# Order at stage edges in a two-layer decoder trunk: PSUM banks of the mLSTM dealt anew, first heads and sums of squares begun some steps later, the last norm's weights on ScalarE

## The chip, the cores and the metric

The kernel runs on one core of a Trainium2 chip. The metric is the device time of one execution in microseconds (us), for which the median of several runs is given. The engines are TensorE (PE in the profile, with its weight loads as PEld), VectorE (DVE), ScalarE (ACT), GpSimd (POOL) and SyncE (SP, which issues most of the weight transfers). Each runs its own instructions in a fixed order and waits for the others by semaphores. TensorE writes into eight PSUM banks of 128 x 512 fp32.

## The reference

512 tokens of width 1024 run through two layers, then a last RMSNorm. Everything is fp32.

```python
def rmsnorm(x, g):
    y = xf * lax.rsqrt(jnp.mean(xf * xf, axis=-1, keepdims=True) + EPS)
    return (y * g.astype(jnp.float32)).astype(x.dtype)

def sqrelu_mlp(h, w1, w2):
    return jnp.square(jax.nn.relu(h @ w1)) @ w2
...
    for layer in range(DEPTH):
        if layer % N_MIXERS == 0:
            mix = diff_attention(rmsnorm(h, attn_norm[j]), ...)
        else:
            mix = mlstm_mixer(rmsnorm(h, mlstm_norm[j]), ...)
        h = h + mix.astype(h.dtype)
        h = h + sqrelu_mlp(rmsnorm(h, mlp_norm[layer]), mlp_w1[layer], mlp_w2[layer]).astype(h.dtype)
    return rmsnorm(h, final_norm)
```

The differential attention has 8 heads of two score maps each (width 64), a softmax with a bias by relative position, the difference of the two maps times the values, and a norm per head. The mLSTM has 4 heads of width 128 for q and k (after a causal convolution of width 4 and SiLU) and 256 for the values, with input and forget gates, a norm per head and an output gate. The MLP's inner width is 4096.

## The kernel before

Activations lie with the features on the partitions: `h[k]`, k = 0 to 7, is 128 features x 512 tokens. An fp32 product is made of three matmuls on rounded halves: an operand is split into a high part `hi` (a ScalarE copy) and a rest `lo` (a VectorE subtraction), and hi x hi, lo x hi and hi x lo are added up in a bank. `mm3` (L400 to L402) does so for 512 tokens at a time, `vpair_mm` (L432 to L434) for products with the tokens on the partitions, `down` (L922 to L924) for the second product of the MLP, and `finish` (L1285 to L1287) for its last 256 features together with the last norm. The weights come as tiles `raw`, and are split into `whi` (ScalarE) and `wlo` (VectorE, L528) ahead of their use.

RMSNorm is not applied before a product but after it. `operand` (L508 on) multiplies `h[k]` with the norm's weights while it splits it into `x_xh` (ScalarE) and `x_xl` (VectorE, L513), and `square_in` (L518) squares `h[k]` on ScalarE and adds it to `acc` on POOL (L524). `token_scale` later splits `acc` into `sh` and `sl`, sums over the partitions with two matmuls with a constant (`sums`, L535 and L536), and makes `rs`, the factor of each token, from the sum: VectorE L559, three ScalarE steps, VectorE L552, L553 and L561. The products are multiplied with `rs` when they are read out of the banks. For products with tokens on the partitions `token_cols` transposes `rs` (L569).

The order of TensorE is the program's. Most products call `tick()` after each step (three matmuls), and `after(n, fn)` runs `fn` n ticks later, so that scores, sums and transposes are put between the steps of the big products. The constants T_... are such distances: T_RS for the sums of the attention's norm, T_RSC for its transposes, T_CONST for L636 to L682 (the bias table's rows and the heads' mixing factors, with a transfer `rows` between), T_ONE and T_TWO for the first two heads' scores (L730), T_M and T_H for the first mLSTM head and the distance between heads, T_MRS for the sums of the mLSTM's norm. The orders of VectorE, ScalarE, POOL and SyncE are set by a scheduler when the kernel is built, so a moved matmul can move their instructions too; at run time they are fixed.

`banks(mm=3, sc=2, ac=3)` deals the eight PSUM banks to three uses: `mm` for products, `sc` for scores and sums, `ac` for what is summed up longer. The list it deals from, `idle`, has the bank that was given out longest ago first. Within a use the banks go round. `four(True)`, with which the mLSTM's gate products begin (`vpair_mm(x, 264)`), takes one `mm` bank and the three `ac` banks.

In the mLSTM's `head`, L1106 spreads the gates into a bank, VectorE (L1109) and ScalarE read it into `e_e`, POOL masks it, L1117 to L1119 make the scores, and VectorE multiplies both (L1120). L1140 on are the products with the values.

In the last MLP `finish` takes the place of the last `down`. It makes the last 256 features of the sum `h` tile by tile (two tiles, j = 0 and 1, for two halves of the tokens, i = 0 and 1). `early_sums` puts the sums of squares of the other 768 features (L1249, L1250) into two banks; `tail` adds those of the last 256, and `scaled` (L1262 on) makes the factor and multiplies. The norm's weights, times -0.5, are multiplied into `h` in between: six whole tiles in L1253 and the last two in halves in L1258.

Of the kernel before, what the change touches and what calls it, by code (L numbers as in the profile page):

```python
# [14 lines left out]
AF = mybir.ActivationFunctionType  # L15
ALU = mybir.AluOpType
# [6 lines left out]
KT = D // P  # L23
# [15 lines left out]

T_RS, T_RSC, T_CONST, T_BIAS, T_ROWS = 24, 39, 31, 4, 14
T_ONE, T_TWO = 3, 12


D_ATT = [
# [8 lines left out]
]  # L55


T_M, T_H = 15, 22
D_MLS = [(5, 8, 6), (5, 7, 9), (5, 9, 10), (7, 8, 12)]

T_GATES, T_GROWS, T_GCOLS, T_MRS = 3, 22, 56, 9
# [124 lines left out]
def trunk(ctx: ExitStack, tc, xT, wgt, wgt2, cols, rows, rel, consts, outT):  # L186
# [18 lines left out]
    def banks(**tags):  # L205

        free = list(idle)
        for tag, n in tags.items():
            turn[tag], free = free[:n], free[n:]
# [15 lines left out]
    mm = nc.tensor.matmul  # L225
    vec = nc.vector
    pool = nc.gpsimd
# [22 lines left out]
    def act(out, x, func, **kw):  # L250
        name = {AF.Exp: LNSET, AF.Ln: LNSET, AF.Sigmoid: SGSET}.get(func)
        if name:
            tables(name)
        ins = nc.scalar.activation(out, x, func, **kw)  # L254
        if name:
            behind(ins, loaded["load"])
            loaded["uses"].append(ins)
# [238 lines left out]
    def col(c):  # L496
        return colt[:, c : c + 1]
# [17 lines left out]
            square_in(k, acc)  # L515
        return lambda: (hi, lo)

    def square_in(k, acc):  # L518
        if k == 0:
            act(acc, h[k], AF.Square)  # L520
        else:
            s = tmp()
            act(s, h[k], AF.Square)
            pool.tensor_tensor(acc, acc, s, op=ALU.add)  # L524

    def split(src, hi, lo, eng=None):
        act(hi, src, AF.Copy)
# [35 lines left out]
    def scale_tile(name):  # L563
        return cp.tile([P, T], F32, tag=name, name=nm(name))
# [276 lines left out]
    def mlp(x, acc, g0, finish=None):  # L841
        with ExitStack() as st:
# [49 lines left out]
            def down(q, i):  # L892
# [53 lines left out]
                for n in (2 * i, 2 * i + 1):  # L946
                    if g0 is not None:
                        nxt.append(operand(n, g0, nacc))
                    else:
                        if n == 0:  # L950
                            finish.acc = acc_tile()
                        square_in(n, finish.acc)

            after(T_MLP, lambda: token_scale(acc, rs))
            ps = group_mm(x)
# [24 lines left out]

    def mlstm(x, acc):
        with ExitStack() as st:
            banks(mm=3, sc=2, ac=3)
            gp = Buffers(tc, st, name="gp", bufs=1)
            qp = Buffers(tc, st, name="qp", bufs=16)
            sg = Buffers(tc, st, name="sg", bufs=8)
# [248 lines left out]
    def finish(operands):  # L1235
# [10 lines left out]
        def early_sums():  # L1246
            split(acc, sh, sl)
            for s, c in zip(stat, (slice(0, H), slice(H, T))):
                mm(s[:, :H], ones_d, sh[:, c], start=True, stop=False)  # L1249
                mm(s[:, :H], ones_d, sl[:, c], start=False, stop=False)  # L1250

        for k in range(KT - 2):
            vec.tensor_scalar(h[k], h[k], col(C_FN + k), -0.5, op0=ALU.mult, op1=ALU.mult)  # L1253

        def tail(n, c, s):
            vec.tensor_tensor(h[n][:, c], part[n - pair[0]][:, c], h[n][:, c], op=ALU.add)
            act(s, h[n][:, c], AF.Square)
            vec.tensor_scalar(h[n][:, c], h[n][:, c], col(C_FN + n), -0.5, op0=ALU.mult, op1=ALU.mult)  # L1258

        def scaled(c, stat, ss):  # L1260
            for s in ss:
# [16 lines left out]
        for i, c in enumerate((slice(0, H), slice(H, T))):  # L1278
            ss = [tmp()[:, :H] for _ in pair]
            for j, n in enumerate(pair):  # L1280
                hi, lo = units[j]
                for k in range(KT):
                    w = slice(k * P, (k + 1) * P)
                    a, b = operands(k, i)
                    mm(part[j][:, c], hi[:, w], a, start=k == 0, stop=False)  # L1285
                    mm(part[j][:, c], hi[:, w], b, start=False, stop=False)
                    mm(part[j][:, c], lo[:, w], a, start=False, stop=k == KT - 1)  # L1287
                    tick()
                tail(n, c, ss[j])
                if i == 0 and j == 0:  # L1290
                    early_sums()
            if i == 0:
                after(T_FIN, lambda c=c, ss=ss: scaled(c, stat[0], ss))
            else:
                scaled(c, stat[1], ss)
# [94 lines left out]
```

## Time and profile before

| | us |
|---|---|
| runs | 1194.72, 1195.81, 1197.52 |
| median | 1195.81 |
| the profiled execution's own time | 1194.34 |
| its span, with a mean TensorE clock of 0.983 | 1192.3 |
| VectorE busy, 77% of the span | 919.9 |
| ScalarE busy, 51% | 603.0 |
| POOL busy, 16% | 189.2 |

The page's other rows of use are those that cut the span into 40 slices; each digit is a busy share in tenths, and PEclk is the clock that TensorE was granted:

```profile
PE   7899999999999999999989899999999999999994
PEclk9899999999999999999989999999999999999997
```

A slice is some 30 us. TensorE is busy nearly everywhere; the slices below 9 are the first two, the last, and the 21st and 23rd, around 610 and 670 us. A busy share of 9 at a clock of half speed is also lost time, which is why both rows are read together. The four places that the change touches are the start of the attention (26 to 60 us), the step from the first MLP to the mLSTM (593 to 617), the mLSTM's heads (640 to 805) and the last norm (1157 to 1192).

### The profile page before, as it was taken

How to read it: one execution, taken by the hardware profiler on the slowest of the kernel's cores; microseconds unless marked ns; L12 is line 12 of the kernel's file. 1: busy time of each engine (PE TensorE's matmuls, PEld its weight loads, DVE VectorE, ACT ScalarE, POOL GpSimd, SP SyncE). 2: the span in 40 equal slices, each digit the busy share in tenths (PEclk: the TensorE clock that was granted, in tenths of full speed). 3: DMA queues.
4: the chain of work that ended last, by engine and by line, in shares of the span. 5: the costliest groups of instructions: out<-in, count | busy, mean ns of one | idle time of the engine just before them, and what ended most of it. 6: DMA issues, size and time to landing. Idle time of an engine off the chain costs nothing.

```text
span 1192.3 us, 17221 instructions
## 1 busy us (share of the span) xinstructions
PE 1147.5 (96%) x6730; PEld 1011.2 (85%) x6730; DVE 919.9 (77%) x1387; ACT 603.0 (51%) x909; POOL 189.2 (16%) x180
## 2 busy tenths in 40 slices
PE   7899999999999999999989899999999999999994
PEld 5778888888998998989877789888889889899894
DVE  7789888587967957867989857766697686786884
ACT  5577776564534534434544537654453353443441
POOL 4432332130000000000221312223000000000011
PEclk9899999999999999999989999999999999999997
DMA  6622222233263362461222221223325526426312
GB/s 202 198 71 71 75 85 71 71 124 111 66 190 112 89 176 89 111 191 53 83 71 70 76 83 54 57 85 107 110 84 136 171 67 162 139 67 185 89 32 71
DMA packets 36592, 123.91 MB, mean 104 GB/s; under 512 B 4351, under 2 KB 6418, under 8 KB 36512
## 3 DMA queue, kind: packets, MB, share of 16 engines
q1 hardware_dynamic: 30288, 103.38, 27.0%
q0 software_dynamic: 5104, 17.87, 7.7%
q10 hardware_dynamic: 1120, 1.57, 0.4%
q8 instruction: 53, 0.87, 0.3%
q14 instruction: 27, 0.22, 0.1%
HBM read 108.11 MB, written 4.74 MB: 95 GB/s over the span
## 4 chain that ended last, share of the span: by engine, by line
PE 78%; DVE 14%; ACT 3%; issue 3%; DMA 2%; POOL 1%; DVEq 0%; SPq 0%; POOLq 0%; ACTq 0%
PE bank L401 15%; PE bank L402 15%; PE bank L400 15%; PE bank L923 7%; PE bank L924 7%; PE bank L922 7%; DVE wlo L528 2%; PE bank L432 2%; PE bank L433 1%; PE bank L434 1%; DVE tmp_tmp L1030 1%; DMA raw<-wgt 1%; DVE x_xl L513 1%; PE bank L730 1%; ACT whi L254 1%
## 5 line engine op out<-in xcount | busy, mean ns | idle before, releaser
L402 PE MATMUL bank<-x_xh,wlo 128*128 128x512 f32 x640 | 255.4, 399 | 1.3 <-DVE wlo L528 1.3
L401 PE MATMUL bank<-x_xl,whi 128*128 128x512 f32 x640 | 254.8, 398 | 1.0 <-DVE x_xl L513 1.0
L400 PE MATMUL bank<-x_xh,whi 128*128 128x512 f32 x640 | 254.0, 397 | 1.4 <-ACT whi L254 1.4
L254 ACT ACTIVATE whi<-raw 128x1024 fp32r<-128x1024 f32 (+2 forms) x128 | 133.4, 1042 | 120.9 <-PE bank L923 48.1
L528 DVE TENSOR_TENSOR wlo<-raw,whi 128x1024 fp32r<-128x1024 f32 (+2 forms) x128 | 161.9, 1265 | 35.2 <-ACT whi L254 34.6
L922 PE MATMUL bank<-uh,whi 128*128 128x256 f32 x560 | 157.9, 282 | 0.0
L924 PE MATMUL bank<-uh,wlo 128*128 128x256 f32 x560 | 157.8, 282 | 0.0
L923 PE MATMUL bank<-ul,whi 128*128 128x256 f32 x560 | 157.8, 282 | 0.0
L400 PEld LDWEIGHTS bank<-x_xh,whi 128*128 128x128 f32 x640 | 122.8, 192 | 28.8 <-ACT whi L254 2.1
L402 PEld LDWEIGHTS bank<-x_xh,wlo 128*128 128x128 f32 x640 | 121.1, 189 | 29.3 <-DVE wlo L528 2.4
L401 PEld LDWEIGHTS bank<-x_xl,whi 128*128 128x128 f32 x640 | 121.5, 190 | 28.3 <-DVE x_xl L513 1.4
L922 PEld LDWEIGHTS bank<-uh,whi 128*128 128x128 f32 x560 | 106.0, 189 | 0.1
L923 PEld LDWEIGHTS bank<-ul,whi 128*128 128x128 f32 x560 | 105.7, 189 | 0.3
L924 PEld LDWEIGHTS bank<-uh,wlo 128*128 128x128 f32 x560 | 105.8, 189 | 0.0
L943 POOL DMA_DIRECT2D h<-work x24 | 20.8, 866 | 511.1 <-DVE work L940 391.5
L254 ACT ACTIVATE uh<-chains 128x1792 fp32r<-128x1792 f32 (+1 forms) x35 | 55.6, 1590 | 57.8 <-DVE chains L883 57.7
L528 DVE TENSOR_TENSOR ul<-chains,uh 128x1792 fp32r<-128x1792 f32 (+1 forms) x35 | 66.0, 1886 | 23.7 <-ACT uh L254 23.4
L524 POOL TENSOR_TENSOR acc_acc<-acc_acc,tmp_tmp 128x512 f32<-128x512 f32 x33 | 54.6, 1654 | 170.8 <-ACT tmp_tmp L254 169.7
L432 PE MATMUL bank<-whi,x_xh 128*128 128x256 f32 (+1 forms) x256 | 73.9, 289 | 7.1 <-DVE work L939 5.7
L876 DVE SCALAR_TENSOR_TENSOR tmp_tmp<-bank,rs_rs 128x512 f32<-128x512 f32 x64 | 44.1, 689 | 45.9 <-PE bank L402 45.5
L254 ACT ACTIVATE whi<-wsums 128x1024 fp32r<-128x1024 f32 x47 | 49.8, 1059 | 51.5 <-PE bank L923 30.3
L433 PE MATMUL bank<-wlo,x_xh 128*128 128x256 f32 (+1 forms) x256 | 73.0, 285 | 0.0
(302 smaller groups left out, 2669.6 us busy)
## 6 DMA issues: line engine op xcount, KB each, us to landing
raw<-wgt SPq DMA_DIRECT2D x156, 512.0 KB, 3.7
rawx<-wgt SPq DMA_DIRECT2D x32, 512.0 KB, 4.2
h<-work POOLq DMA_DIRECT2D x24, 512.0 KB, 5.8
skew<-frd POOLq DMA_DIRECT2D x8, 320.0 KB, 7.3
bias_bias<-skew POOLq DMA_DIRECT2D x8, 256.0 KB, 3.1
outT<-h SPq DMA_DIRECT2D x6, 256.0 KB, 2.5
raw<-wgt SPq DMA_DIRECT2D x2, 528.0 KB, 3.6
h<-xT ACTq DMA_DIRECT2D x4, 256.0 KB, 4.9
```

The source lines that it names most:

```text
L254: ins = nc.scalar.activation(out, x, func, **kw)
L400: mm(ps, whi, x[0], start=first, stop=False)
L401: mm(ps, whi, x[1], start=False, stop=False)
L402: mm(ps, wlo, x[0], start=False, stop=last)
L432: mm(ps, xh, hi[:, c], start=k == 0, stop=False)
L433: mm(ps, xh, lo[:, c], start=False, stop=False)
L524: pool.tensor_tensor(acc, acc, s, op=ALU.add)
L528: (eng or vec).tensor_tensor(lo, src, asf(hi), op=ALU.subtract)
L876: vec.scalar_tensor_tensor(m, p, 0.0, rs, op0=ALU.max, op1=ALU.mult)
L922: mm(out[name], hi[:, n], uh[:, t], start=first, stop=False, skip_group_check=late)
L923: mm(out[name], hi[:, n], ul[:, t], start=False, stop=False, skip_group_check=late)
L924: mm(out[name], lo[:, n], uh[:, t], start=False, stop=k == 3, skip_group_check=late)
```

## The change

Five things are changed, all in the order of work; the numbers computed are the same products and sums.

- T_RS goes from 24 to 28, T_ONE from 3 to 7 and T_TWO from 12 to 9: the attention's sums and its first head's scores come four ticks later, its second head's one tick later. T_RSC and T_CONST stay.
- T_M goes from 15 to 21 and T_H from 22 to 21: the four mLSTM heads come 6, 5, 4 and 3 ticks later. T_MRS stays.
- The mLSTM's banks are dealt in the order ac, mm, sc, so that the first ones of the list go to `ac`.
- In the last MLP the squares of tiles 4 and 5 are added up on VectorE rather than POOL.
- In `finish` the weights times -0.5 are made once (`gain`), the six whole tiles are multiplied on ScalarE, and `early_sums` comes behind the second tile's 24 matmuls rather than ahead of them. Lines of `finish` from L1253 on have a number that is two higher.

```diff
@@ -39,8 +39,8 @@
 
 
 
-T_RS, T_RSC, T_CONST, T_BIAS, T_ROWS = 24, 39, 31, 4, 14
-T_ONE, T_TWO = 3, 12
+T_RS, T_RSC, T_CONST, T_BIAS, T_ROWS = 28, 39, 31, 4, 14
+T_ONE, T_TWO = 7, 9
 
 
 D_ATT = [
@@ -55,7 +55,7 @@
 ]
 
 
-T_M, T_H = 15, 22
+T_M, T_H = 21, 21
 D_MLS = [(5, 8, 6), (5, 7, 9), (5, 9, 10), (7, 8, 12)]
 
 T_GATES, T_GROWS, T_GCOLS, T_MRS = 3, 22, 56, 9
@@ -515,13 +515,13 @@
             square_in(k, acc)
         return lambda: (hi, lo)
 
-    def square_in(k, acc):
+    def square_in(k, acc, eng=None):
         if k == 0:
             act(acc, h[k], AF.Square)
         else:
             s = tmp()
             act(s, h[k], AF.Square)
-            pool.tensor_tensor(acc, acc, s, op=ALU.add)
+            (eng or pool).tensor_tensor(acc, acc, s, op=ALU.add)
 
     def split(src, hi, lo, eng=None):
         act(hi, src, AF.Copy)
@@ -949,7 +949,7 @@
                     else:
                         if n == 0:
                             finish.acc = acc_tile()
-                        square_in(n, finish.acc)
+                        square_in(n, finish.acc, vec if i == 2 else pool)
 
             after(T_MLP, lambda: token_scale(acc, rs))
             ps = group_mm(x)
@@ -980,7 +980,7 @@
 
     def mlstm(x, acc):
         with ExitStack() as st:
-            banks(mm=3, sc=2, ac=3)
+            banks(ac=3, mm=3, sc=2)
             gp = Buffers(tc, st, name="gp", bufs=1)
             qp = Buffers(tc, st, name="qp", bufs=16)
             sg = Buffers(tc, st, name="sg", bufs=8)
@@ -1249,13 +1249,15 @@
                 mm(s[:, :H], ones_d, sh[:, c], start=True, stop=False)
                 mm(s[:, :H], ones_d, sl[:, c], start=False, stop=False)
 
+        gain = scale_tile("rs2")[:, :KT]
+        vec.tensor_scalar(gain, colt[:, C_FN : C_FN + KT], -0.5, None, op0=ALU.mult)
         for k in range(KT - 2):
-            vec.tensor_scalar(h[k], h[k], col(C_FN + k), -0.5, op0=ALU.mult, op1=ALU.mult)
+            act(h[k], h[k], AF.Copy, scale=gain[:, k : k + 1])
 
         def tail(n, c, s):
             vec.tensor_tensor(h[n][:, c], part[n - pair[0]][:, c], h[n][:, c], op=ALU.add)
             act(s, h[n][:, c], AF.Square)
-            vec.tensor_scalar(h[n][:, c], h[n][:, c], col(C_FN + n), -0.5, op0=ALU.mult, op1=ALU.mult)
+            vec.tensor_scalar(h[n][:, c], h[n][:, c], gain[:, n : n + 1], None, op0=ALU.mult)
 
         def scaled(c, stat, ss):
             for s in ss:
@@ -1287,7 +1289,7 @@
                     mm(part[j][:, c], lo[:, w], a, start=False, stop=k == KT - 1)
                     tick()
                 tail(n, c, ss[j])
-                if i == 0 and j == 0:
+                if i == 0 and j == 1:
                     early_sums()
             if i == 0:
                 after(T_FIN, lambda c=c, ss=ss: scaled(c, stat[0], ss))
```

**VectorE at the start of the attention.** Each row is a line of the program, the operation, and what it writes and reads; `sl_sl` is the rest of the sum of squares, `bank_83` the bank of the sums, `coef` the heads' mixing factor, and `rs_rs_183` the tokens' factor. Before:

```order
L528 TENSOR_TENSOR sl_sl_333<-acc_acc_128,sh_sh_332 128x512
L559 TENSOR_SCALAR chains<-bank_83 128x512
L528 TENSOR_TENSOR wlo_94<-raw_88,whi_91 128x1024
L667 TENSOR_TENSOR tmp_tmp_233<-tmp_tmp_204 128x128
L674 TENSOR_REDUCE tmp_tmp_255<-tmp_tmp_233 128x2
L552 TENSOR_TENSOR chains<-chains 128x512
L680 TENSOR_TENSOR tmp_tmp_255<-tmp_tmp_255 128x1
L553 SCALAR_TENSOR_TENSOR chains<-chains 128x512
L682 TENSOR_SCALAR coef<-tmp_tmp_255 128x1 x2
L561 TENSOR_SCALAR rs_rs_183<-chains 128x512
```

In the changed kernel:

```order
L528 TENSOR_TENSOR sl_sl_348<-acc_acc_128,sh_sh_347 128x512
L528 TENSOR_TENSOR wlo_94<-raw_88,whi_91 128x1024
L667 TENSOR_TENSOR tmp_tmp_233<-tmp_tmp_204 128x128
L674 TENSOR_REDUCE tmp_tmp_255<-tmp_tmp_233 128x2
L680 TENSOR_TENSOR tmp_tmp_255<-tmp_tmp_255 128x1
L682 TENSOR_SCALAR coef<-tmp_tmp_255 128x1 x2
L559 TENSOR_SCALAR chains<-bank_83 128x512
L552 TENSOR_TENSOR chains<-chains 128x512
L553 SCALAR_TENSOR_TENSOR chains<-chains 128x512
L528 TENSOR_TENSOR wlo_92<-raw_86,whi_89 128x1024
L561 TENSOR_SCALAR rs_rs_183<-chains 128x512
```

L559, the first step from the sums to `rs`, stood ahead of L667 and now stands behind it and its followers, and a weight split (`wlo_92`) has come between L553 and L561.

**TensorE at the first gate products of the mLSTM.** `whi` and `wlo` are gate weights, `x_xh` and `x_xl` the activations, `sh_sh` and `sl_sl` the two parts of the sum of squares. These are the rows around the sums. Before:

```order
L432 MATMUL bank_84<-whi_89,x_xh_239 128x264
L433 MATMUL bank_84<-wlo_92,x_xh_239 128x264
L434 MATMUL bank_84<-whi_89,x_xl_240 128x264
L535 MATMUL bank_77<-sh_sh_332,ones_d 128x512
L536 MATMUL bank_77<-sl_sl_333,ones_d 128x512
L432 MATMUL bank_82<-whi_89,x_xh_239 128x264
```

In the changed kernel:

```order
L432 MATMUL bank_80<-whi_89,x_xh_239 128x264
L433 MATMUL bank_80<-wlo_92,x_xh_239 128x264
L434 MATMUL bank_80<-whi_89,x_xl_240 128x264
L535 MATMUL bank_82<-sh_sh_347,ones_d 128x512
L536 MATMUL bank_82<-sl_sl_348,ones_d 128x512
L432 MATMUL bank_81<-whi_89,x_xh_239 128x264
```

The four banks of these products, in their order, were 80, 84, 82 and 83 and are now 77, 80, 81 and 79; 82 had held the last product of the MLP's `down`. The sums have gone from bank 77 to 82 and stand behind the same 54 matmuls as before.

**VectorE at the first score matmuls of the mLSTM.** `wlo` are weight splits, `vl` rests of value tiles, `e_e` the gates' factors of the first chunk. Before:

```order
L1030 SCALAR_TENSOR_TENSOR tmp_tmp_204<-conv_5080,colt,tmp_tmp_204 128x512
L582 SCALAR_TENSOR_TENSOR vl_1_v_5628<-bank_80,rscol_rscol_472,vh_1_v_5626 128x256
L1037 TENSOR_TENSOR tmp_tmp_233<-tmp_tmp_204,tmp_tmp_233 128x512
L1109 TENSOR_SCALAR e_e_5680<-bank_78,rc 128x128
L528 TENSOR_TENSOR wlo_92<-raw_86,whi_89 128x1024
L1120 TENSOR_TENSOR e_e_5680<-bank_77,e_e_5680 128x512
```

In the changed kernel:

```order
L582 SCALAR_TENSOR_TENSOR vl_1_v_5628<-bank_77,rscol_rscol_472,vh_1_v_5626 128x256
L1037 TENSOR_TENSOR tmp_tmp_233<-tmp_tmp_204,tmp_tmp_233 128x512
L528 TENSOR_TENSOR wlo_92<-raw_86,whi_89 128x1024
L582 SCALAR_TENSOR_TENSOR vl_1_v_5629<-bank_78,rscol_rscol_472,vh_1_v_5627 128x256
L528 TENSOR_TENSOR wlo_93<-raw_87,whi_90 128x1024
L582 SCALAR_TENSOR_TENSOR vl_1_v_5629<-bank_78,rscol_rscol_472,vh_1_v_5627 128x256
L1109 TENSOR_SCALAR e_e_5708<-bank_83,rc 128x128
L1120 TENSOR_TENSOR e_e_5708<-bank_82,e_e_5708 128x512
```

L1109 stood ahead of the two weight splits and the two last value tiles and now stands behind all four.

## The prediction

> **What bounds the kernel now.** I read the page's engine rows first, then TensorE's waits, then the timeline around each large wait.
>
> ```profile
> PE 1147.5 (96%) x6730; PEld 1011.2 (85%) x6730; DVE 919.9 (77%) x1387; ACT 603.0 (51%) x909; POOL 189.2 (16%) x180
> ...
> PE bank L432 <- DVE work L939: 5.7, 1, 5.7
> PE bank L1249 <- ACT sh_zeros L254: 5.1, 1, 5.1
> PE bank L1106 <- ACT e_e L254: 3.9, 1, 3.9
> PE bank L730 <- DVE vl_v L582: 3.1, 2, 2.4
> PE bank L536 <- DVE sl_sl L528: 1.9, 1, 1.9
> ...
> PE bank L432 <- DVE work L937: 1.4, 1, 1.4
> ```
>
> TensorE is busy for 96% of the span, and the change takes no matmul away, so time can only come from its waits and from its clock. The longest waits (total, times, longest) stand at four places: the attention's start (L536, L730), the step from the first MLP to the mLSTM (L432), the mLSTM's first head (L1106) and the last norm (L1249). Each is paid twice, because the clock is half after it. Two stretches of equal length behind the 5.7 us wait show that (the last columns are the granted clock and DMA):
>
> ```profile
> 601.80:606.80 5.00, 4.94 (x22) 4.94 (x23) 4.93 (x12) 2.38 (x4) 1.62 (x1) 0.50 0.01 3
> 606.80:611.80 5.00, 5.00 (x42) 4.91 (x41) 3.94 (x7) 1.69 (x2) 1.62 (x1) 1.00 0.00 0
> 682.90:688.70 5.80, 4.80 (x12) 3.72 (x13) 4.75 (x8) 2.92 (x7) 1.16 (x2) 0.50 0.51 165
> ```
>
> 22 matmuls pass at clock 0.50 where 42 pass at 1.00 (0.12 us each): 20 of them, 2.4 us, are lost. The rows below show half clock for 3.4 us after the 1.9 us wait at L536 (its own 0.80 us at 30.02 is twice the 0.39 of a like one, which is back at 33.49), and the last norm's rows for some 6.4: so 1.7 to 3.2 us go with each long wait. After the 1.4 us wait at L432 the records show none, so the point lies between 1.4 and 1.9. What counts at each edge is which operand comes last there.
>
> **Attention's start: +1.4 us (-1 to +3.3).** PE and DVE, with start and duration:
>
> ```profile
> 30.02 0.80 PE L536 MATMUL bank<-sl_sl,ones_d 128*128 128x512 f32 x1 [1.92 <-DVE sl_sl L528]
> ...
> 33.49 0.39 PE L401 MATMUL bank<-x_xl,whi 128*128 128x512 f32 x1
> ...
> 37.42 0.28 PE L432 MATMUL bank<-whi,x_xh 128*128 128x256 f32 x1
> ...
> 42.36 0.60 PE L569 MATMUL bank<-ident,rs_rs 128*128 128x128 f32 x4
> ```
>
> ```profile
> 29.29 0.67 DVE L528 TENSOR_TENSOR sl_sl<-acc_acc,sh_sh 128x512 fp32r<-128x512 f32 x1
> 30.85 0.69 DVE L559 TENSOR_SCALAR chains<-bank 128x512 f32<-128x512 f32 x1 [0.89 <-PE bank L536]
> ...
> 36.83 0.29 DVE L667 TENSOR_TENSOR tmp_tmp<-tmp_tmp 128x128 f32<-128x128 f32 x1 [4.16 <-DMA tmp_tmp<-rows]
> ...
> 38.81 0.42 DVE L561 TENSOR_SCALAR rs_rs<-chains 128x512 f32<-128x512 f32 x1
> ...
> 31.58 1.95 ACT L254 ACTIVATE chains<-chains 128x512 f32<-128x512 f32 x3 [3.08 <-DVE chains L559]
> ```
>
> T_RS puts the sums 12 matmuls later, 12 times 0.23 or 2.8 us (678.13 to 678.59 further down is two of them), which covers sl_sl (ready 29.96). The 1.92 us wait, its 0.46 us forerunner at L535 and some 1.7 us of half clock go: the group that ended at 37.4 ends near 33.3, -4.1. But VectorE's order changes with it. L559, which begins the chain to rs, used to run at 30.85, in the gap before L667. Now it stands behind L667, and L667 waits for the transfer of the rows until 36.83 whatever PE does. From there: four short steps, which I put at 0.2 each like L667's 0.29 overlapped, to 37.9, L559 0.69, then ScalarE's three chain steps 1.95, L552 and L553 like L559, one wlo split (1.22 in a row further down) that is now put ahead of L561, and L561 0.42: rs comes at about 43.5 and not at 39.23. T_RSC is unchanged, so the transposes L569 still follow 42 matmuls of 0.118 (37.42 to 42.36) and are reached near 38.2. PE waits 5.3 us there, with all value products queued behind, and loses some 2.2 more at half clock: +3.4 with the -4.1.
>
> Some of it is already spent in the two L730 waits (3.1 us) further on. Head 0's scores now follow 12 more 512-column matmuls (T_ONE, 2.8 us), while the bank that the second of them waits for comes 3.1 us later, because rs moved by 4.3 and one split of 1.2 left that stretch. That makes +0.3 there, and up to 1.7 less if the remaining wait falls under the length that halves the clock; the walk is no finer than a microsecond, and I take -0.3. For head 1 the scores come straight behind head 0's transposes, with ScalarE's four kh copies (about 0.63 each, like sh_sh below) ahead of the last copy that frees a bank: between 0 and 2.5, taken as 1.7. Together +1.4.
>
> **First MLP to mLSTM: +2.1 us (+0.3 to +3.2).**
>
> ```profile
> 593.56 0.29 PE L432 MATMUL bank<-whi,x_xh 128*128 128x264 f32 x1
> ...
> 601.86 0.59 PE L432 MATMUL bank<-whi,x_xh 128*128 128x264 f32 x1 [5.68 <-DVE work L939]
> ...
> 610.00 0.39 PE L535 MATMUL bank<-sh_sh,ones_d 128*128 128x512 f32 x1
> ...
> 608.47 0.63 ACT L254 ACTIVATE sh_sh<-acc_acc 128x512 fp32r<-128x512 f32 x1 [2.67 <-POOL acc_acc L524]
> ...
> 609.14 0.69 DVE L528 TENSOR_TENSOR sl_sl<-acc_acc,sh_sh 128x512 fp32r<-128x512 f32 x1 [0.33 <-ACT sh_sh L254]
> ```
>
> The new deal of banks does what it says: the first products go to four banks that VectorE has read out before 593.56, and both L432 waits (1.45 and 5.68) go. What is late next is the sum of squares. L535 stands behind the same 54 matmuls of the gate products (T_MRS is unchanged), and PE reaches it at 593.56 + 54 x 0.12 = 600.0. Its operand comes from POOL's last add (the releaser in the row of sh_sh) and ends at 609.1; sl_sl ends at 609.83. VectorE's and ScalarE's orders here stay almost as they were, and none of these steps waits for a bank that PE now has sooner. So PE waits 9.7 us in one piece instead of 7.1 in two, resumes at 610.3 as before, and now runs the 42 products that are left at half clock. Before, that half clock fell into time that was waited for anyway. It costs 1.7 to 3.2, as above; I take 2.1, between the 3.4 us and 5 us stretches. If the steps up to sl_sl come 1.4 us earlier as well, +0.3 is left.
>
> The Trainium skill, "TensorE: Matmul & The Clock Gate", Part 1 (the HAM clock gate), has the clock halve after an idle window of about 3.4 us and return after about as long of sustained work, counted by a window that runs freely. The 5 us at 0.50 above exceed that. By the rule the term would be 1.7, a little less than mine, and the wait at L536, under 2 us, should not have halved the clock, which it did.
>
> **mLSTM heads: -0.3 us (-3 to +1.5).**
>
> ```profile
> 678.13 0.39 PE L400 MATMUL bank<-x_xh,whi 128*128 128x512 f32 x1
> ...
> 678.59 0.40 PE L402 MATMUL bank<-x_xh,wlo 128*128 128x512 f32 x1
> 682.86 0.69 PE L1106 MATMUL bank<-gs,sel 128*128 128x384 f32 x1 [3.87 <-ACT e_e L254]
> 684.55 0.69 PE L1117 MATMUL bank<-qk_qkh,qk_qkh 128*128 128x384 f32 x1 [1.00 <-DVE e_e L1120]
> ...
> 681.10 1.04 ACT L254 ACTIVATE whi<-raw 128x1024 fp32r<-128x1024 f32 x1
> ...
> 684.80 1.22 DVE L528 TENSOR_TENSOR wlo<-raw,whi 128x1024 fp32r<-128x1024 f32 x1
> ```
>
> T_M moves the first score matmuls 21 rows back and the second L1106 18, which is 18 x 0.23 = 4.2 us of work in the hole. But ScalarE's table load, qk copy and whi (done 682.14) do not move, and VectorE now makes two wlo splits (1.2 each) and two vl_v before L1109, where it had made none. PE now reaches the next weights at 680.9 and waits 1.3 for whi and 0.8 for wlo; L1109 comes near 685.4, the second L1106 at 686.5 (wait 2.2), and L1117, behind it as before by 1.7, at 688.2 against 684.55. 3.65 us later with 4.2 more done: -0.5. The half clock of 682.9 to 688.7, 12 matmuls in 4.8 us or 2.4 lost, becomes some 1.7: -0.7. At the mLSTM's end its last head is 9 rows (2.1 us) later towards an output product that is not, less a split of 1.2 that left that stretch: +0.9. The sum is -0.3.
>
> **Last norm: -7.2 us (-5 to -7.7).**
>
> ```profile
> 1161.79 0.28 PE L1287 MATMUL bank<-uh,wlo 128*128 128x256 f32 x1
> 1167.19 0.58 PE L1249 MATMUL bank<-sh_zeros,ones_d 128*128 128x256 f32 x1 [5.12 <-ACT sh_zeros L254]
> ...
> 1173.65 0.28 PE L1285 MATMUL bank<-sh_sh,whi 128*128 128x256 f32 x1
> ...
> 1162.80 1.46 ACT L254 ACTIVATE tmp_tmp<-h 128x512 f32<-128x512 f32 x3 [4.46 <-DVE h L945]
> 1166.51 0.63 ACT L254 ACTIVATE sh_zeros<-acc_acc 128x512 fp32r<-128x512 f32 x1 [2.25 <-POOL acc_acc L524]
> ...
> 1163.57 2.90 POOL L524 TENSOR_TENSOR acc_acc<-acc_acc,tmp_tmp 128x512 f32<-128x512 f32 x2 [2.63 <-ACT tmp_tmp L254]
> ...
> 1167.17 0.69 DVE L528 TENSOR_TENSOR sl_sl<-acc_acc,sh_zeros 128x512 fp32r<-128x512 f32 x1 [0.55 <-ACT sh_zeros L254]
> ...
> L1253 DVE TENSOR_SCALAR h<-h,colt x6: 474/481/1372, 1157.1 to 1164.0; 128x512 f32<-128x512 f32 x6
> ...
> 603.43 0.72 ACT L254 ACTIVATE x_xh<-h,colt 128x512 fp32r<-128x512 f32 x1 [6.36 <-DVE h L945]
> ```
>
> The 24 matmuls of the second tile (24 x 0.118 = 2.85) now run from 1161.9 to 1164.75, in the time that was waited. The scalings leave VectorE (four at 0.48 ahead of the last h, so that h ends some 1.0 earlier, at 1161.7), and ScalarE, idle 4.46 there, does them at about 0.72, the nearest row with a per-partition factor. The last two adds go from POOL (2.90 for two) to VectorE (0.69 each, like sl_sl): squares to 1162.9, adds to 1163.9, ScalarE's last two scalings and one square to 1164.5, sh to 1165.2, sl to 1165.9. PE waits about 0.5 and 0.6, too little to halve its clock, and begins the second half at 1166.35 instead of 1173.65. Nothing behind changes: -7.2. Should the two waits reach 1.9 us (a wlo or the ScalarE queue late), half clock comes back and 5 are left. The new 128x8 factor is one short VectorE operation long before; I cost it at nothing, since PE reads nothing of it, and at most some 0.2.
>
> The Trainium skill, "ScalarE: Activation LUTs", Rules for kernel authors, sends multiplications to VectorE and not to ScalarE, as the faster per element. The rows agree on the price (0.48 against 0.72). By that rule alone the six would cost 1.4 us, but the row of ScalarE's idle time says where they go.
>
> **Sum.** +1.4 + 2.1 - 0.3 - 7.2 = -4.0 on the profiled execution of 1194.34: 1190.3. The median shown is 1195.81, 1.5 higher, so 1191.8 on its footing.
>
> **Rivals.** *The waits go as the words say*: rs is not delayed (attention -4.1) and the mLSTM's hole of 3.87 + 1.0 + 2.4 is filled (-7.3), while the sums wait at L535 for nothing more than before; with the end -18.6, about 1177; with one of the two places about -10, 1185. Against it stand L667's wait for a transfer and the splits ahead of L1109. *Given back whole*: attention costs its +3.3, the mLSTM start +3.2 and the heads +1.5; with the end about +0.8, and with half of these excesses -1.6: 1194 to 1196.6. *Slower*: VectorE never makes up its 4.3 us in the attention.
>
> ```profile
> sum 120.00, PE 118.23 PEld 102.01 DVE 105.02 ACT 89.68 POOL 40.22; mean PE 19.71 PEld 17.00 DVE 17.50 ACT 14.95 POOL 6.70
> ```
>
> This is the sum row of six stretches of 20 us from 60 to 180. VectorE has 15 us free in 120, so the lag should be gone after some 35 us. If that free time is itself time in which it waits for scores, it isn't, and the short PE waits at the head changes lengthen past the point between 1.4 and 1.9 us; each then costs 1.9 + 1.7. Three of these are +10.8: -4.0 + 10.8, about 1202.6; two, 1199.
>
> **Chances.** Forecast (-2.4 to -8) 0.62, waits gone 0.08, given back 0.23, slower 0.07. A measurement of this kernel tells no less than 0.2%, 2.4 us, from no change, so faster is 0.70, same 0.23, slower 0.07. The range runs from the half of the first rival, 1185.5, to short of the slower one, 1198; the forecast's own is 1187.8 to 1193.4.
>
> **What would show it.** In the changed kernel: no wait at L536 near 30 us but one of 4 to 6 at L569 near 38 us for rs; no L432 wait near 600 us but 8 to 10 at L535, with half clock to 615; L1106's long wait split into several; and no wait over 1.5 us at L1249, with clock 1.0 from 1165 on. The forecast fails if L569 doesn't wait, if the attention keeps its lag beyond 100 us, or if the last norm still halves the clock.

## The result, and the profile after

The changed kernel takes 1204.99 us (median of four runs, 1202.79 to 1206.05) against 1196.57 of the kernel before on the same chip (the median of four runs; the table above has three of them): a ratio of 1.007, with a 95% interval of 1.005 to 1.009. It is 8.4 us slower, where 4 faster was forecast. The profiled execution took 1202.79 us, with a span of 1200.8.

From the page of the changed kernel, the engines and the two slice rows:

```profile
PE 1147.9 (96%) x6730; PEld 1010.4 (84%) x6730; DVE 913.8 (76%) x1384; ACT 606.2 (50%) x915; POOL 183.6 (15%) x178
...
PE   8789999999999999999969998999999999999996
...
PEclk9899999999999999999989999999999999999998
```

TensorE's work is what it was. The last slice went from 4 to 6, the 21st (near 610 us) from 8 to 6. What TensorE waited for (line, releaser, total, times, longest):

```profile
PE bank L535 <- ACT sh_sh L254: 9.1, 1, 9.1
PE bank L569 <- DVE rs_rs L561: 7.2, 1, 7.2
PE bank L1106 <- ACT e_e L254: 5.8, 2, 4.0
PE bank L730 <- DVE ptl L768: 2.1, 1, 2.1
...
PE bank L763 <- DVE e_e L750: 1.5, 1, 1.5
...
PE bank L1250 <- DVE sl_sl L528: 0.3, 1, 0.3
```

The waits named in the prediction at L536, L432 and L1249 are gone or short; L535 and L569 have come in their place, as forecast. L1106 has not shrunk: 5.8 us in two where there were 3.9 in one. To place the loss I add up the matmuls in each trace by their columns (0.231 us for 512, in proportion below that), and compare the times at which the same sum is reached. After minus before, by the time in the trace of before:

| at (us) | after - before | what lies between the row above and this one |
|---|---|---|
| 37 | -4.2 | the attention's sums |
| 48 | +5.5 | L569 waits for rs |
| 64 | +1.1 | first attention head |
| 80 | +5.7 | second attention head |
| 590 | +5.9 | nothing more |
| 615 | +8.2 | first MLP to mLSTM |
| 692 | +6.4 | first mLSTM head |
| 727 | +13.0 | second mLSTM head |
| 735 | +11.2 | third head's first block, where a 1.23 us wait of before (L1117) is gone |
| 780 | +13.9 | rest of the third head, fourth head |
| 810 | +15.7 | output product |
| 1160 | +15.8 | nothing |
| 1174, and the end | +8.4 | last norm |

So the last norm gave 7.5 us, and the attention (5.9), the step to the mLSTM (2.3) and the heads (7.5) took 15.7. The heads' 7.5 are -1.8 at the first, +6.6 at the second, -1.8 where the third begins, +2.7 behind that, and +1.8 at the output product.

**Attention's start.** VectorE and then TensorE of the changed kernel (start, duration, instruction, idle time before it and its releaser):

```profile
38.66 0.29 DVE L667 TENSOR_TENSOR tmp_tmp<-tmp_tmp 128x128 f32<-128x128 f32 x1 [7.46 <-DMA tmp_tmp<-rows]
...
39.93 0.68 DVE L559 TENSOR_SCALAR chains<-bank 128x512 f32<-128x512 f32 x1
...
45.10 0.42 DVE L561 TENSOR_SCALAR rs_rs<-chains 128x512 f32<-128x512 f32 x1
```

```profile
45.57 1.11 PE L569 MATMUL bank<-ident,rs_rs 128*128 128x128 f32 x4 [7.23 <-DVE rs_rs L561]
...
71.63 0.59 PE L763 MATMUL bank<-ident,e_e 128*128 128x128 f32 x3 [1.48 <-DVE e_e L750]
74.32 0.70 PE L730 MATMUL bank<-kh_kh,q_q 128*128 128x512 f32 x1 [2.10 <-DVE ptl L768]
```

L559 stands behind L667, and L667 behind the transfer of the rows: rs comes at 45.5 where 43.5 was forecast, 1.8 of it because the transfer landed at 38.66 and not at 36.83. The second head then costs 4.6: the first head's transposes ahead of it (L763) wait 1.48 us for the last e_e, and its scores (L730) 2.10 for the bank, with half clock behind them. VectorE shows why the bank came late:

```profile
70.99 0.85 DVE L750 SCALAR_TENSOR_TENSOR e_e<-e_e,sm_sm,e_onehot 128x256 f32<-128x256 f32 x2 [0.71 <-POOL e_onehot L748]
71.76 0.68 DVE L704 TENSOR_TENSOR tmp_tmp<-bank,rs_rs 128x512 f32<-128x512 f32 x1
72.36 1.21 DVE L528 TENSOR_TENSOR wlo<-raw,whi 128x1024 fp32r<-128x1024 f32 x1
73.49 1.47 DVE L768 TENSOR_TENSOR ptl<-bank,pth 128x512 fp32r<-128x512 f32 x3
```

Between the last e_e and the ptl that frees the bank stand two instructions for other work, 1.9 us together. In the kernel before, the split stood there too, but TensorE came to the transposes only when e_e was ready and waited 0.8 us in all:

```profile
68.09 0.47 PE L730 MATMUL bank<-kh_kh,q_q 128*128 128x512 f32 x1 [0.80 <-DVE ptl L768]
```

**The mLSTM's second head.** ScalarE of the kernel before and of the changed one, at the third of the head's four score blocks (e_e is the gate's exponential, L245 loads ScalarE's function table):

```profile
716.93 0.29 ACT L254 ACTIVATE e_e<-e_e 128x128 f32<-128x128 f32 x1
717.13 0.35 ACT L254 ACTIVATE e_e<-bank,rc 128x128 f32<-128x128 f32 x1
...
718.83 1.28 ACT L245 ACT_TABLE_LOAD   x1
720.12 2.19 ACT L254 ACTIVATE sig_sig<-sig_sig 128x512 f32<-128x512 f32 x4
```

```profile
727.47 1.28 ACT L245 ACT_TABLE_LOAD   x1
728.76 0.63 ACT L254 ACTIVATE chains<-chains 128x512 f32<-128x512 f32 x1
729.30 2.18 ACT L254 ACTIVATE sig_sig<-sig_sig 128x512 f32<-128x512 f32 x4
731.50 1.28 ACT L245 ACT_TABLE_LOAD   x1
733.45 0.63 ACT L254 ACTIVATE qk_qkh<-of_of 128x512 fp32r<-128x512 f32 x1 [0.67 <-POOL of_of L1179]
734.68 0.63 ACT L254 ACTIVATE qk_qkh<-of_of 128x512 fp32r<-128x512 f32 x1 [0.59 <-POOL of_of L1179]
735.21 0.29 ACT L254 ACTIVATE e_e<-e_e 128x128 f32<-128x128 f32 x1
735.41 0.35 ACT L254 ACTIVATE e_e<-bank,rc 128x128 f32<-128x128 f32 x1
```

And TensorE of the changed kernel:

```profile
726.25 0.28 PE L1106 MATMUL bank<-gs,sel 128*128 128x256 f32 x1
...
735.81 0.39 PE L1106 MATMUL bank<-gs,sel 128*128 128x256 f32 x1 [3.96 <-ACT e_e L254]
```

Before, e_e ran ahead of the first table load. Now the head is five ticks later and e_e stands behind both table loads, four sigmoids and two copies: its block was spread into the bank at 726.25 and is read at 735.41. The next block's L1106 needs that bank and waits 3.96 us, with its scores (another 0.49) and the products of L432 queued behind it. From 735.8 to 740.0 the granted clock is 0.59 on average, and the 16 matmuls in that stretch lose some 1.9 us to it: 6.3 us of the 6.6 in the table.

**The end.** TensorE of the changed kernel at the last norm: L1249 follows the products without a wait.

```profile
1180.86 0.38 PE L1249 MATMUL bank<-sh_zeros,ones_d 128*128 128x256 f32 x1
1181.58 0.38 PE L1250 MATMUL bank<-sl_sl,ones_d 128*128 128x256 f32 x1 [0.34 <-DVE sl_sl L528]
```

### The profile page after: what moved, and what is told of

The parts are those of the page before. It is cut to its first block, busy times and chain, and to the rows that moved or that the text cites. A ratio compares the mean times of both kernels' runs of the same rounds, so it can differ in the third digit from the quotient of the medians.

```text
span 1200.8 us, 17227 instructions
## 1 busy us (share of the span) xinstructions
PE 1147.9 (96%) x6730; PEld 1010.4 (84%) x6730; DVE 913.8 (76%) x1384; ACT 606.2 (50%) x915; POOL 183.6 (15%) x178
## 5 line engine op out<-in xcount | busy, mean ns | idle before, releaser
L402 PE MATMUL bank<-x_xh,wlo 128*128 128x512 f32 x640 | 255.1, 399 | 2.0 <-DVE wlo L528 2.0
L400 PE MATMUL bank<-x_xh,whi 128*128 128x512 f32 x640 | 253.4, 396 | 1.9 <-ACT whi L254 1.9
L400 PEld LDWEIGHTS bank<-x_xh,whi 128*128 128x128 f32 x640 | 122.3, 191 | 29.7 <-ACT whi L254 3.1
L402 PEld LDWEIGHTS bank<-x_xh,wlo 128*128 128x128 f32 x640 | 121.0, 189 | 30.2 <-DVE wlo L528 3.6
L524 POOL TENSOR_TENSOR acc_acc<-acc_acc,tmp_tmp 128x512 f32<-128x512 f32 x31 | 52.0, 1677 | 167.9 <-ACT tmp_tmp L254 166.8
L432 PE MATMUL bank<-whi,x_xh 128*128 128x256 f32 (+1 forms) x256 | 74.8, 292 | 0.0
```

The lines of the kernel that those rows point to most:

```text
L400: mm(ps, whi, x[0], start=first, stop=False)
L402: mm(ps, wlo, x[0], start=False, stop=last)
L432: mm(ps, xh, hi[:, c], start=k == 0, stop=False)
L524: (eng or pool).tensor_tensor(acc, acc, s, op=ALU.add)
```

## The experiments

Each kernel was run beside the kernel before on its own chip. Ratios to that kernel have their 95% interval; microseconds are (ratio - 1) x 1196.

### The four parts, each alone

The first has only the T_ constants of the attention.

```diff
-T_RS, T_RSC, T_CONST, T_BIAS, T_ROWS = 24, 39, 31, 4, 14
-T_ONE, T_TWO = 3, 12
+T_RS, T_RSC, T_CONST, T_BIAS, T_ROWS = 28, 39, 31, 4, 14
+T_ONE, T_TWO = 7, 9
```

> Only the attention's constants are changed (T_RS 28, T_ONE 7, T_TWO 9). Theory: the four edges are independent, and the trace's +5.9 us between the starts of the two programs and 64 to 190 us comes from these constants alone: 0.5% slower than before, about +5.9 us, with L569 waiting 5 to 8 us for rs and a wait of 2 us or more at the second head's first L730. Rival: part of the 5.9 us is the day's transfer of the rows (36.8 us before, 38.7 after), which the constants do not set: then L667 would be back near 36.8 and the loss about +4.

1.0028 (1.0017 to 1.0038), +3.3 us. L569 waits 6.7, and the second head's 1.5 and 2.1 are there too.

```diff
-            banks(mm=3, sc=2, ac=3)
+            banks(ac=3, mm=3, sc=2)
```

> Only the mLSTM's deal of banks is changed. Theory: it costs what the step between 593 and 615 us shows, +2.3 us (one wait of 9 us or more at L535 in place of the two at L432, and half clock behind it), and nothing in the heads: +2.3. Rival: the new deal also makes the heads' waits (scores and products use other banks in turn), so that most of the +7.5 us between 672 and 810 us comes from here: +6 to +10.

1.0009 (0.9999 to 1.0019), +1.1 us, which can't be told from nothing. Its trace has the L535 wait (9.09) and loses 1.9 between 590 and 615 us.

```diff
-T_M, T_H = 15, 22
+T_M, T_H = 21, 21
```

> Only T_M (21) and T_H (21) are changed. Theory: the +7.5 us between 672 and 810 us come from these two: ScalarE's exponentials of a chunk of the second head stand behind the first head's output steps, which wait for POOL. About +7.5 us, with a wait of some 4 us at an L1106 near 730 and waits at the output product's first use of the last head. Rival (the deal of banks makes them): -2 to +1.

1.0082 (1.0067 to 1.0097), +9.8 us. The first head gains 2.7 in its trace; then 7.7 go at the second head, where L1106 waits 3.97 for e_e behind the same table loads, and 4.7 from there to the output product.

The fourth has only the parts for the last norm: the squares of tiles 4 and 5 added on VectorE, and the changes in `finish`.

```diff
+            (eng or pool).tensor_tensor(acc, acc, s, op=ALU.add)
...
+            act(h[k], h[k], AF.Copy, scale=gain[:, k : k + 1])
...
+                if i == 0 and j == 1:
                     early_sums()
```

> Only the last norm is changed (early_sums behind the second tile, the weights on ScalarE, two adds on VectorE). Theory: the gain of the trace at the end, -7.5 us, stands by itself: about 0.6% faster, with no wait over 1 us at L1249. Rival: in the changed kernel the end gained because ScalarE and VectorE reached it in another state; then less than -5.

0.9949 (0.9935 to 0.9964), -6.1 us; in the trace -7.5 between 1160 and 1174 us. The four add up to +8.1, against +8.4 for the changed kernel: within the intervals no dependence between the parts is seen, and the heads are the largest.

### What the waits hang on

Attention constants, with the rows' step two ticks later, so that L559 isn't behind L667:

```diff
-T_RS, T_RSC, T_CONST, T_BIAS, T_ROWS = 24, 39, 31, 4, 14
-T_ONE, T_TWO = 3, 12
+T_RS, T_RSC, T_CONST, T_BIAS, T_ROWS = 28, 39, 33, 4, 14
+T_ONE, T_TWO = 7, 9
```

> The attention's three constants as changed, and T_CONST 33 in place of 31, which puts L667 and its followers behind L559 to L561 on VectorE; nothing else differs. Theory (L667's wait for the rows, ahead of L559, makes the new wait at L569): rs comes near 36 us, L569 waits under 1 us, and 5 to 7 us of waiting and 1.7 us of half clock go against the run with the three constants alone; what is left of its +3 us against before is -3 to +0.5, the wait at the second head's first L730 (4 us with its half clock) being the open part. Rival (the later first heads are what costs): L569's wait goes, but the time lands within 1 us of the run with the three constants, since the heads wait instead.

1.0008 (0.9997 to 1.002), +1.0 us. From its VectorE and POOL timelines:

```profile
36.79 0.42 DVE L561 TENSOR_SCALAR rs_rs<-chains 128x512 f32<-128x512 f32 x1
...
48.98 0.29 DVE L667 TENSOR_TENSOR tmp_tmp<-tmp_tmp 128x128 f32<-128x128 f32 x1 [6.66 <-DMA tmp_tmp<-rows]
```

```profile
40.45 3.04 POOL L713 TENSOR_TENSOR q_q<-tmp_tmp,q_q 64x512 fp32r<-64x512 f32 x2
43.78 0.57 POOL L666 DMA_DIRECT2D tmp_tmp<-rows  x1 [0.30 <-POOL q_q L713]
```

rs comes 8.3 us sooner and the L569 wait is gone, so L667 was what rs stood behind. But the rows' transfer is now issued behind POOL's work on q at 43.78, L667 blocks VectorE until 48.98, and the first head's L730 waits 4.75. The wait went along with L667, and the time lies between what was expected with the wait gone and what the rival would have.

The new deal of banks, with the gate products and their sums later:

```diff
-T_GATES, T_GROWS, T_GCOLS, T_MRS = 3, 22, 56, 9
+T_GATES, T_GROWS, T_GCOLS, T_MRS = 13, 26, 58, 21
...
-            banks(mm=3, sc=2, ac=3)
+            banks(ac=3, mm=3, sc=2)
```

> The mLSTM's new deal of banks, and its sums of squares 12 ticks later (T_MRS 21, behind all gate products and 15 matmuls of the next), with the readers behind them (T_GATES 13, T_GROWS 26, T_GCOLS 58). Theory (the new banks take 7.1 us of waits away, and the sums of squares at the same place took them back): the wait at L535 falls from 9 us to under 1.5, a wait of 2 to 3 us is left at L569 for rs, and the time is 3 to 5 us under the run with the banks alone, -2 to -4 against before. Rival (the whole mLSTM hangs on rs, so what is won at L535 is waited for at L569 or at the products' banks): within 1 us of the run with the banks alone, +0.5 to +2.

0.9978 (0.9964 to 0.9992), -2.6 us, 3.7 below the deal alone. No wait is left at L535 in the mLSTM; its trace gains 4.5 from 590 to 615 us and gives 3.1 back by 692, in waits of 1.4 to 2.4 us at L569, L400 and L402. On the way the first head's L1106, the wait that the later T_M was to fill, falls from 3.87 to 0.35 us without any change to T_M.

The heads later, and the sigmoids six ticks later as well, so that the table loads come behind e_e again:

```diff
-T_M, T_H = 15, 22
+T_M, T_H = 21, 21
...
-T_SIG = 2
+T_SIG = 8
```

> T_M and T_H as changed, and T_SIG 8 in place of 2: the four sigmoids, with their two table loads, come six ticks later too, so that on ScalarE the third chunk's exponentials of the second head stand ahead of them again. Theory (that pile ahead of e_e makes the wait of 4 us at the fifth L1106): this wait goes, 5 to 6 us of the +9.5 us with it, +3 to +5 against before are left (later waits of the last heads and at the output product). Rival (the second head's gates come late on VectorE or POOL in any case): within 1.5 us of the run with the two constants alone, +8 to +11.

1.0008 (0.9997 to 1.0019), +1.0 us: 8.8 below the later heads alone. ScalarE of this kernel:

```profile
717.45 0.29 ACT L254 ACTIVATE e_e<-e_e 128x128 f32<-128x128 f32 x1
...
718.17 0.35 ACT L254 ACTIVATE e_e<-bank,rc 128x128 f32<-128x128 f32 x1
718.53 1.28 ACT L245 ACT_TABLE_LOAD   x1
```

e_e is ahead of the table load and the 4 us wait is gone: by 735 us this trace is 4.6 ahead of the kernel before, and from 692 to 727, where the later heads alone lose 7.7, it loses nothing. It gives that back in waits of 0.6 to 0.8 us in the third and fourth head and 1.8 at the output product.

The same, with the heads one tick closer together (21, 20), to save the output product:

> As the run before it, and T_H 20 in place of 21, so that the heads come 6, 4, 2 and 0 ticks later than before the change. Theory (what is left there is the last heads' lateness, some 2.7 us of waits in their chunks and 3.3 at the output product's first use of the last head): with the last head at its old place 3 to 5 us less than the run with T_H 21 and T_SIG 8, -2 to +1 against before, since the first head's gain of 2.7 us stays. Rival (the waits come from the heads being packed more closely): not faster than that run, +3 or more.

1.0 (0.9984 to 1.0015), no gain that can be told from the last. The output product does lose 1.6 less in the trace, but 3.4 go between 735 and 780 us, where 2.7 went. The two traces also differ ahead of that, by 2.6 us at 735.

Is it the later sigmoids themselves, or their meeting with the later heads? The kernel before, with T_SIG alone:

```diff
-T_SIG = 2
+T_SIG = 8
```

> The kernel before with T_SIG 8 in place of 2, T_M and T_H as before. Theory (the sigmoids cost only where the heads' new places put their exponentials behind them): -2 to +1, since at the old places the third chunk stood ahead of them already; so some 7 to 9 us of what T_SIG 8 gained belong to T_M and T_H. Rival (T_SIG 2 is a bad place in any case): -5 or less.

1.002 (1.0007 to 1.0033), +2.4 us, above the -2 to +1 of the theory and far from the rival's gain. By themselves the later sigmoids cost: TensorE's timeline has

```profile
734.85 0.50 PE L1117 MATMUL bank<-qk_qkh,qk_qkh 128*128 128x512 f32 x1 [3.16 <-ACT rs_rs L254]
```

where before it was 1.23. The place of table loads and sigmoids against the heads decides, not either alone.

### The rows' transfer

The rows are constants and can be loaded at the start, into a tile of their own. With the constants of before:

```diff
+            rowt = ap_.tile([P, 256], F32, name="rowt")
             def bias_table():
+                nc.gpsimd.dma_start(rowt, row_of(0, 256))
...
-                rowt, prod = tmp(), tmp()
-                nc.gpsimd.dma_start(rowt[:, :256], row_of(0, 256))
+                prod = tmp()
```

> The kernel before, with the transfer of the rows that L667 reads issued at tick 4 into a tile of its own, ahead of everything that POOL's queue then waits for, so that L667 no longer waits on VectorE. All constants as before. Theory (the wait of L667 stands on the path from the sums to rs): rs comes near 36 us and not at 39 to 41, both L730 waits of the first head shrink, -2 to -5 us; and the first 60 us differ less from run to run. Rival (the first head waits for its bias or its value tiles in any case): within 1.5 us of before.

0.9988 (0.9978 to 0.9997), -1.4 us. L667 (here L669, two lines on) starts sooner, but still waits:

```profile
33.32 0.29 DVE L669 TENSOR_TENSOR tmp_tmp<-rowt 128x128 f32<-128x128 f32 x1 [2.74 <-DMA frd<-tmp_tmp]
```

Its result goes to a buffer out of which another transfer (frd) is still reading. The ten runs lie within 2.9 us, the 19 of the kernel before within 4.8.

The same with the attention's three new constants:

> The attention's three constants as changed (T_RS 28, T_ONE 7, T_TWO 9), and the early transfer of the rows as in the run above; T_CONST stays at 31. Theory (the constants cost only because L559 came behind L667's wait): no wait at L569 and none at L536, the first head's L730 waits under 1 us, -3 to -8 us against before, and below the run with the early rows alone. Rival (the order of the first two heads costs by itself, through the second head's first L730): the wait of 2 us with its half clock stays there and the time is the same as or above that of the run with the early rows alone.

0.9993 (0.9983 to 1.0003), -0.8 us. Against the first part alone that is 4.1 less. Its trace is 3.7 ahead at 64 us and loses 4.6 at the second head, in the waits at L763 and L730 of the changed kernel.

Two more kernels take this apart. One has T_RS at 28 and the rows early, but T_ONE and T_TWO as before:

> T_RS 28 and the early rows; T_ONE and T_TWO as before. It differs from the run of all three constants with early rows in the first two heads' places alone. Theory (the second head's wait is the price of T_ONE and T_TWO): no wait at an L763 or L730 between 60 and 75 us above 1 us, and 3 to 5 us less than that run, -3 to -6 against before. Rival (the late rs makes it): the wait is there again, within 1.5 us of that run.

0.9991 (0.9982 to 1.0001), -1.1 us. The second head's wait is as short as before (0.80), so T_ONE and T_TWO made it. But the first head's L730 now waits 3.76 and 0.76, and the time is that of the last kernel within 0.3 us, not the 3 to 5 less that were expected. Where the heads are put decides which one waits.

The other has all three constants, the rows early, and tiles of their own for L667's result and the sums behind it:

```diff
+            prod = ap_.tile([P, P], F32, name="prod")
...
+                dots = ap_.tile([P, 4], F32, name="dots")
```

> The three constants as changed, early rows, and tiles of their own for the product and the sums that L667 and L674 write, so that nothing of them waits for a transfer under way. Theory (L667 and L674 hold up L559): rs comes near 36 us (40.3 with the shared tiles, 45.1 as changed), L569 and L730 of the first head wait under 0.5 us, and 1 to 3 us go against the run with the shared tiles; the second head's wait of 2 us stays. Rival (the first head waits for its transfers of the bias): no change.

0.9985 (0.9974 to 0.9997), -1.8 us. The wait at L569 is gone, the first head's are under 1 us, and from 25 to 64 us the trace gains 8.3. The second head still costs 5.5. And in the kernel's first 12 us TensorE waits 5.6 for x_xl, which no kernel without these tiles does; why they move the start was not followed.

### What beats both

The last norm's part, the banks with later sums, and the rows early, with the attention and the heads as before:

```diff
+T_GATES, T_GROWS, T_GCOLS, T_MRS = 13, 26, 58, 21
...
+            banks(ac=3, mm=3, sc=2)
...
+                nc.gpsimd.dma_start(rowt, row_of(0, 256))
...
+            act(h[k], h[k], AF.Copy, scale=gain[:, k : k + 1])
```

> The three parts that gain by themselves, put together: the changed last norm (-6 by its own run), the new banks with the sums of squares and their readers later (-2.6), and the early rows with the attention's constants of before. Theory (the edges are independent): the sum of the three runs, -10 to -14 us against before. Rival (they meet somewhere): less than -8.

1186.07 us, 0.9921 (0.9906 to 0.9936): 9.4 us faster than the kernel before, of the 10.1 that the parts give by themselves. TensorE's longest waits in it:

```profile
PE bank L400 <- DVE vl_v L582: 2.6, 2, 1.8
PE bank L402 <- DVE wlo L528: 2.4, 1, 2.4
PE bank L732 <- DVE vl_v L582: 2.3, 1, 2.3
```

The same with the attention's constants of the change:

> As the run before it, with the attention's three constants as changed. Theory: the sum of the parts again, with the run of the constants and early rows in place of the early rows alone, -11 to -17 us against before. Rival (the second head's wait takes it back): no faster than the run before it.

0.9924 (0.9907 to 0.994): they bring nothing here either.

And one with T_RS at 28, the two own tiles and T_SIG at 8 on top of the best:

> The changed last norm, the new banks with later sums of squares, T_RS 28, early rows with tiles of their own, and T_SIG 8; first heads and mLSTM heads at their places of before. Theory (independent edges): some 3 to 6 us under the best run so far (-9.4), -12 to -16 against before. Rival (the gain of the attention or of the sigmoids is lost at the next edge): -8 to -11.

0.9937 (0.9915 to 0.996), -7.5 us, short of the rival's -8 and no better than the best (the intervals overlap): its trace has the 5.2 us wait for x_xl at the start and loses 3.1 between 727 and 750 us, as with the later sigmoids alone.

## Why the prediction was wrong

Between the forecast of -4.0 us and the trace of the changed kernel lie 12.4; 7.8 of them are the mLSTM heads, 4.5 the attention.

**The step that failed is the mLSTM heads**, put at -0.3 us within -3 to +1.5; they cost 7.5 in the trace and, alone, 9.8. The first head was walked, and held: -1.8 measured against -1.2 (-0.5 of waits and -0.7 of half clock). But T_M moves four heads, and the other three were taken as moved without harm. For the second, the question that the first head got (what stands ahead of e_e on ScalarE?) was not asked, although the trace of before showed that its e_e ended only 1.35 us ahead of a table load. That is the +6.6 at 727 us, and the run with both the heads and the sigmoids later, where e_e is ahead of the load again, shows it. The last head's +0.9 at the output product was +1.8. The 2.7 in the third and fourth head, with three waits of 0.6 to 0.8 us, were not foreseen either. That T_SIG at 8 is slower alone rules out that it is simply a better place.

**Attention: +1.4 forecast, +5.9 in the trace, +3.3 alone.** The mechanism was right: L559 behind L667, L667 behind the rows, L569 waiting. The sums gained 4.2 (4.1 forecast). Two terms were mis-sized: L569 with its half clock took 9.6 and not 7.5, as the transfer landed later, and the second head cost 4.6 and not 1.7. The first head gave 4.3 back where 3.7 were forecast (the -0.3 of the prediction is the balance behind that head, -4.1 + 7.5 - 3.7). For the second head the prediction named ScalarE's kh copies as what holds the bank, and the trace shows VectorE's e_e and the split ahead of ptl. The trace probably overstates this part (+5.9 against +3.3 alone): the kernel before was profiled in an execution in which the transfer landed at 36.83, and kernels with the same code up to there had it as late as 40.17 (below).

**First MLP to mLSTM: +2.1 forecast, +2.3 in the trace.** Both L432 waits went, L535 waits 9.1 us in one piece and L536 another 0.4 (9.7 forecast), and the half clock now falls on products. Alone it is +1.1, with 2.1 inside its interval. The Trainium skill, "TensorE: Matmul & The Clock Gate", Part 1, asks for one busy window of about 3.4 us before full clock returns, and that window runs freely. The trace agrees as far as it goes: matmuls are at full spacing again at 620.6, 5.3 us after L535 started, more than one such window and less than two. The loss at half clock is 1.5 to 1.7.

**Last norm: -7.2 forecast (its own times, 1173.65 and 1166.35, give -7.3), -7.5 in the trace, -6.1 alone.** The waits came at 0 and 0.3 us where 0.5 and 0.6 were forecast, the clock stays up, and TensorE waits for none of the scalings on ScalarE (0.71 us each).

**The rivals.** The slower rival had the sign and came nearest in size (+3.2 to +6.8 against +8.4), with the prices of an added wait beyond 1.9 us plus half clock. Its mechanism was another, VectorE lagging through the attention: from 80 to 590 us the difference stays between 4.9 and 6.5, so such a lag cost nothing there. The kernel lost in the attention's first heads and mostly in the mLSTM's, by the order on VectorE and ScalarE, and the rival's size is luck. "The waits go as the words say" is not true of the change. In the best version it holds in part: the waits at the first mLSTM head's L1106 and at the last norm's early sums are down to 0.34 us, and the longest at L432 is 1.8, but L536 still waits its 1.9.

Left open: T_M and T_H were not tried apart.

## What to carry to other kernels

When one constant moves several stages, walk each of them: for every moved matmul, look up on each engine what the instruction that frees its bank now stands behind, table loads above all. A wait that hides behind an operand (a transfer, a sum, a bank) goes where that operand is read: look where it comes out next before it is counted as gone. L667 later only moved its wait, while the mLSTM's sums later were worth 3.7 us behind the new banks. And profile the parts alone: here one good part of four was worth 6 us and was buried under the others.

## What the runs showed of the hardware

The landing of one small transfer differs from run to run, with the same instructions ahead of it. VectorE's L667, in kernels whose code up to there is the same:

```profile
36.22 0.29 DVE L667 TENSOR_TENSOR tmp_tmp<-tmp_tmp 128x128 f32<-128x128 f32 x1 [4.10 <-DMA tmp_tmp<-rows]
```

```profile
39.27 0.29 DVE L667 TENSOR_TENSOR tmp_tmp<-tmp_tmp 128x128 f32<-128x128 f32 x1 [6.82 <-DMA tmp_tmp<-rows]
```

The first is the new deal of banks alone, the second the later heads alone; the kernel before had 36.83, and the others like it lie between 35.61 and 40.17. The transfer itself took 3.7 to 5.6 us from its issue to L667; the rest is the issue, which stood between 31.79 and 34.55, behind another transfer (frd). TensorE's time at 64 us goes along, from -0.9 to +4.3 against the trace of before. A single trace's difference of 2 us downstream of such a wait says little; the medians do.

The same wait is followed by half clock in one execution and not in another. The prediction read a point between 1.4 and 1.9 us out of the trace of before, where L536's 1.92 us wait (its row at 30.02) is followed by half clock, 0.51 from 30.0 to 33.4. In the run with the new banks and later sums the same wait is as long, and the clock stays at 1.00 from 30.6 to 34.0:

```profile
30.62 0.50 PE L536 MATMUL bank<-sl_sl,ones_d 128*128 128x512 f32 x1 [1.92 <-DVE sl_sl L528]
30.95 0.40 PE L400 MATMUL bank<-x_xh,whi 128*128 128x512 f32 x1
```

So a wait of this length costs half clock in some executions and not in others, with the same code ahead of it; the point between 1.4 and 1.9 us does not hold, and what decides it was not followed.

In the changed kernel a change of table takes 1.28 us on ScalarE and no more: the load at 727.47 is followed by an activation at 728.76, 0.01 us after its end. The Trainium skill, "ScalarE: Activation LUTs", What ACT_TABLE_LOAD costs, gives 2.66 us with a drain, which these rows don't show. The price was not the load itself but all that it stands ahead of.
